# Strassen's seven products in the output projection, with weight sums made by adding DMAs

## The chip, the core and the metric

The kernel runs on one core of a Trainium2 chip. The metric is the device time of one execution, in microseconds (us). The median of three runs of the kernel before is 950.04 us (949.63 to 950.85).

## What is computed

A hybrid encoder block on x (1 x 512 x 2048, float32): adaLN-modulated RMSNorm, one input projection, dilated attention and a gated linear attention side by side, each times a SiLU gate. The change concerns what comes behind them:

```python
y = jnp.concatenate([a_out, g_out], axis=-1) @ w_out[layer]     # (512 x 2048) @ (2048 x 2048)
x = x + gate[:, None] * y
return rms_norm(x) * final_gain
```

## The kernel before, in words

Everything is float32, and a product is made of three matmuls in the `fp32r` form: each operand is split into a high half (rounded to that form) and a low half (what is left), and `three` (L205 to L208) adds high x high, low x high and high x low in PSUM. The high half of a weight tile is an ACT copy (L385), the low half a DVE subtraction (L369).

**The work in stages.** `unit` makes one projection of 512 output columns: four row or column tiles, 16 k tiles, three matmuls each, 192 matmuls of 128 x 512. The order of the units is qk2, qk4, qk6, gk, gv0, gv1, ag0, ag1, gg0, gg1 and then o0 to o3, the output projection. TensorE's order is the program's (`manual_schedule` for PE); DVE, ACT, POOL and SP are put in order by a scheduler, by priorities and dependencies, and `urgent` raises the priority of work that is put beside a unit (`side`, with the point in the unit at which each piece is issued).

**Weights.** A tile of weights is 128 x 2 x 512 (512 KB, two k tiles). `fetch` loads it from SP's queue into one of four ring slots (`raw`); `split_hi` and `split_lo` make the halves in one of three slots each (`whi`, `wlo`). A raw slot is free when the low half is made, a split slot when its last matmul is done. In a unit of the output projection one such tile feeds 24 matmuls (four row tiles x two k tiles x three), some 5.4 us.

**The operand.** The mixed and gated activations lie in four tiles `cat[0..3]`, 128 x 4 x 512 each: `cat[0]` and `cat[1]` are the attention half of the contraction (k tiles 0 to 7), `cat[2]` and `cat[3]` the other half. `cat_split` makes their halves: those of `cat[0]` and `cat[1]` beside the unit gg1, those of the others behind it, into the `h` tiles that held the normalised input (free when gg1 is done).

**The output.** After each of o0 to o2, `add_up` takes four PSUM tiles: DVE multiplies by the gate row `sb` (L1118) and adds x (L1119), ACT squares and sums (L1121), POOL multiplies by the final gain (L1123). The unit o3 runs as row tiles (0, 1), then 2, then 3, so that `finish` (ln, exp, scaling by DVE, ACT and POOL, four stores of 256 KB) of one lies beside the matmuls of the next; `finish_last` is what stands behind the last matmul. Five weight tiles of o3 are split early and kept.

**Queues.** SP issues all loads and stores but a few, in order; an issue that waits holds those behind it. POOL issues two small DMAs (L331) near the start. `gate_row` turns the gate into a row: a transposition on TensorE, an eviction by ACT, a DMA to memory and one back to all partitions (`sb`, 1 MB).

Of the kernel before, what the change touches and what calls it, by code (L numbers as in the profile page):

```python
# [18 lines left out]
P = 128  # L19
# [97 lines left out]

def _plan(tasks, free, ready):
# [52 lines left out]
def block_kernel(ctx: ExitStack, tc: tile.TileContext, a: dict):  # L171
# [5 lines left out]
    t2 = ctx.enter_context(tc.tile_pool(name="t2", bufs=16))  # L177
    gp = ctx.enter_context(tc.tile_pool(name="gp", bufs=2))
    sm = ctx.enter_context(tc.tile_pool(name="sm", bufs=4))
# [25 lines left out]
    def three(ps, lh, ll, rh, rl, first, last):  # L205
        mm(ps, lh, rh, start=first, stop=False)  # L206
        mm(ps, ll, rh, start=False, stop=False)  # L207
        mm(ps, lh, rl, start=False, stop=last)  # L208
# [111 lines left out]
    def row_part(j, i):  # L320
# [9 lines left out]
        if i:  # L330
# [6 lines left out]
    order = ["qk2", "qk4", "qk6", "gk", "gv0", "gv1", "ag0", "ag1", "gg0", "gg1",  # L337
             "o0", "o1", "o2", "o3"]
    gorder = [0, 1, 2, 3, 7, 4, 5, 6]
    uses = [(u, g) for u in order for g in (gorder if u == "o3" else range(KT // 2))]  # L340
    early = [("o3", g) for g in (0, 1, 2, 3, 7)]
    groups = []
    for u, g in uses:
        if (u, g) not in early:
            groups.append((u, g))
        if u == "o2" and 1 <= g <= 5:
            groups.append(early[g - 1])
    gi = {ug: i for i, ug in enumerate(groups)}
    upto = {}
    for i, ug in enumerate(uses):  # L350
        upto[ug] = max([gi[x] for x in uses[:i + 2]])
    raws, wts, low, c_h = {}, {}, set(), []

    def fetch(i):
        if i < len(groups) and i not in raws:
            u, g = groups[i]
            raws[i] = RAW(f"raw_{u}{g}", [2, 512])
            nc.sync.dma_start(raws[i], a["w_" + u][g])
# [13 lines left out]
    def split_hi(i):  # L372
        if i < len(groups) and i not in wts:
            fetch(i)
            u, g = groups[i]
            raw = raws[i].rearrange("p k c -> p (k c)")
            if u == "o3" and g < 4:
                dst = [t[:, 8 + 2 * g:10 + 2 * g, :].rearrange("p k c -> p (k c)") for t in c_h]
            elif u == "o3" and g == 7:
                dst = [gp.tile([P, 1024], F32R, tag="g", name=f"{u}{g}{e}") for e in "hl"]  # L380
            else:
                dst = None
            wts[i] = dst or (wp.tile([P, 1024], F32R, tag="whi", name=f"{u}{g}h"),
                             wp.tile([P, 1024], F32R, tag="wlo", name=f"{u}{g}l"))
            act(wts[i][0], raw, AF.Copy)  # L385
# [564 lines left out]
    def unit(name, natural, side=(), rhs=None, lr=None, tiles=range(4)):  # L950
# [3 lines left out]
        ps = [PJ(f"ps_{name}_{i}") for i in tiles]  # L954
        pos, tick, ticks = 0, 0, 16 * len(tiles)
        for q in range(KT // 2):
            g = gorder[q] if name == "o3" else q
            i0 = gi[name, g]
            todo = []
            if 0 in tiles:  # L960
                todo = list(range(gi[name, gorder[0] if name == "o3" else 0], upto[name, g] + 1))
                for i in todo:
                    split_hi(i)
                for ahead in (1, 2):
                    fetch(upto[name, g] + ahead)
            if i0 not in low:
                split_lo(i0)
            hi, lo = wts[i0]
            for n, i in enumerate(tiles):
                for kk in range(2):  # L970
                    k = 2 * g + kk
                    rh, rl = (h_hi[:, k, :], h_lo[:, k, :]) if rhs is None else rhs[k]
                    if natural:
                        t = slice(i * P, i * P + P)
                        cw = slice(kk * 512, kk * 512 + 512)
                        three(ps[n], rh[:, t], rl[:, t], hi[:, cw], lo[:, cw], q + kk == 0, q + kk == KT // 2)
                    else:
                        c = slice(kk * 512 + i * P, kk * 512 + i * P + P)
                        three(ps[n], hi[:, c], lo[:, c], rh, rl, q + kk == 0, q + kk == KT // 2)
                    tick += 1  # L980
                    if tick % (2 * len(tiles)) == 2:
                        for i_ in todo:
                            split_lo(i_)
# [5 lines left out]
            for i_ in todo:  # L989
                split_lo(i_)  # L990
# [77 lines left out]
    rhs = {}  # L1068

    def cat_split(k, hi, lo):  # L1070
        src = cat[k // 4][:, k % 4, :]
        act(hi, src, AF.Copy)
        tt(lo, src, hi.bitcast(F32), op=ALU.subtract)
        rhs[k] = (hi, lo)

    cs = []
    for j in range(2):
        cs.append((B8(f"ch{j}", [4, 512], F32R), B8(f"cl{j}", [4, 512], F32R)))
    side = [(0.1 + 0.08 * k, (lambda k=k: cat_split(k, cs[k // 4][0][:, k % 4, :], cs[k // 4][1][:, k % 4, :])))
            for k in range(8)]  # L1080
    ps = unit("gg1", False, side + some_sums("gg1"))
    gate_evict(ps, cat[3], "g1")
    for e in "hl":
        c_h.append(hp.tile([P, KT, 512], F32R, tag="h", name="c_" + e))
    for k in range(8):
        cat_split(8 + k, c_h[0][:, k, :], c_h[1][:, k, :])

    def gate_row():
# [3 lines left out]
        gt_ = sm.tile([KT, P], F32, tag="oh", name="gatet", bufs=1)  # L1092
        act(gt_, pg[:KT, :P], AF.Copy)
        garow = dp.tile([KT, P], F32, tag="garow", name="garow")
        nc.sync.dma_start(garow, gt_)
        nc.sync.dma_start(sb, bass.AP(garow.tensor, garow.offset, [[0, P], [1, D]]))

    x2, fgain = [], []
# [3 lines left out]
    def x_again(i):  # L1102
        def go():
            x2.append(B8(f"x2_{i}", [4, 512]))
            nc.sync.dma_start(x2[i].rearrange("p k c -> p (k c)"), a["x"][i * P:i * P + P, :])
        return go

    def gain_row(j):
        def go():
            fgain.append(T2(f"fgain{j}"))  # L1110
            nc.sync.dma_start(fgain[j], bass.AP(a["fgain"].tensor, a["fgain"].offset + 512 * j, [[0, P], [1, 512]]))
        return go

    def add_up(i, ps, j):

        x_ = x2[i][:, j, :]
        t = T2(f"y{i}{j}")
        tt(t, ps, sb[:, 512 * j:512 * j + 512], op=ALU.mult)  # L1118
        tt(x_, t, x_, op=ALU.add)  # L1119
        sq = T2(f"ysq{i}{j}")  # L1120
        act(sq, x_, AF.Square, accum_out=ssq[:, i, j:j + 1])  # L1121
        if j < 3:
            nc.gpsimd.tensor_tensor(x_, x_, fgain[j], op=ALU.mult)  # L1123

    for j in range(3):
        side = [(0.1 + 0.2 * i, x_again(i)) for i in range(4)] if j == 0 else []
        if j == 0:
            side += [(0.08, gate_row)] + [(0.15 + 0.2 * i, gain_row(i)) for i in range(4)]
        ps = unit(f"o{j}", True, side, rhs=rhs)
        for i in range(4):  # L1130
            add_up(i, ps[i], j)
    for i in range(4):

        tt(ssq[:, i, 0:1], ssq[:, i, 0:1], ssq[:, i, 1:2], op=ALU.add)
        tt(ssq[:, i, 0:1], ssq[:, i, 0:1], ssq[:, i, 2:3], op=ALU.add)
        nc.vector.tensor_scalar(ssq[:, i, 0:1], ssq[:, i, 0:1], 1.0 / D, EPS, op0=ALU.mult, op1=ALU.add)

    def finish(i, ps):

        add_up(i, ps, 3)  # L1140
        r = rn[:, i:i + 1]
        act(r, ssq[:, i, 3:4], AF.Ln, bias=ssq[:, i, 0:1], scale=1.0 / D)
        act(r, r, AF.Exp, scale=-0.5)
        x_ = x2[i]
        stt(x_[:, 3, :], x_[:, 3, :], r, fgain[3], op0=ALU.mult, op1=ALU.mult)
        act(x_[:, 0, :], x_[:, 0, :], AF.Copy, scale=r)
        nc.gpsimd.tensor_scalar(x_[:, 2, :], x_[:, 2, :], r, 1.0, op0=ALU.mult, op1=ALU.mult)
        act(x_[:, 1, :], x_[:, 1, :], AF.Copy, scale=r)
        for z in (3, 0, 2, 1):
            nc.sync.dma_start(a["out"][i * P:i * P + P, 512 * z:512 * z + 512], x_[:, z, :])  # L1150

    def finish_last(i, ps):

        add_up(i, ps, 3)
        r, x_ = rn[:, i:i + 1], x2[i]
        act(r, ssq[:, i, 3:4], AF.Ln, bias=ssq[:, i, 0:1], scale=1.0 / D)
        act(r, r, AF.Exp, scale=-0.5)

        def store(queue, z):
            queue.dma_start(a["out"][i * P:i * P + P, 512 * z:512 * z + 512], x_[:, z, :])  # L1160

        nc.vector.tensor_scalar(x_[:, 1, :], x_[:, 1, :], r, None, op0=ALU.mult)
        store(nc.sync, 1)
        act(x_[:, 0, :], x_[:, 0, :], AF.Copy, scale=r)
        stt(x_[:, 3, :], x_[:, 3, :], r, fgain[3], op0=ALU.mult, op1=ALU.mult)
        store(nc.sync, 0)
        act(x_[:, 2, :], x_[:, 2, :], AF.Copy, scale=r)
        store(nc.scalar, 2)
        store(nc.sync, 3)

    for tiles in ((0, 1), (2,), (3,)):
        ps = unit("o3", True, rhs=rhs, tiles=tiles)
        for i, p_ in zip(tiles, ps):
            if i < 3:
                finish(i, p_)
    with tc.manual_schedule(engines=PLANNED):
        finish_last(3, ps[0])
# [71 lines left out]
```

## Time and profile before

| | us |
|---|---|
| runs, median (lowest to highest) | 950.04 (949.63 to 950.85) |
| profiled execution, span from its first to its last instruction | 948.1 |
| first matmul of the output projection, from the span's start | 765.08 |
| last matmul | 939.09 |

The own time of the profiled execution isn't listed beside its span; the median of the runs is 1.9 us above the span. In the profile PE is TensorE's matmuls and PEld its weight loads (which overlap them), DVE is VectorE, ACT ScalarE, POOL GpSimd and SP the engine that issues most DMAs. A group's row gives line, engine, operation, output <- input, shape, count, then busy us and mean ns of one, then the idle time in front of it and what ended it. A row of the timeline begins with its start and its duration. L numbers are lines of the kernel before. In the windows, each engine's busy us and count of instructions are followed by the granted clock of TensorE (1.00 is full), the mean busy share of the 16 DMA engines and GB/s.

### The profile page before, as it was taken

The numbers are of one execution on the slowest core, as the hardware profiler recorded it, in microseconds if no ns is written. First come the engines' busy times: TensorE is split into PE (matmuls) and PEld (weight loads), VectorE is DVE, ScalarE is ACT, GpSimd is POOL, SyncE is SP. The second block draws the span as 40 slices with busy tenths as digits, with TensorE's granted clock in tenths as the row PEclk, the third lists the DMA queues.
The fourth block names the chain that finished last, engine by engine and source line by source line (L and its number), as shares of the span: only waits on it lengthen the run. The fifth ranks groups of instructions, "written<-read, shape, count | busy, mean of one in ns | idle before, by whom it ended". The sixth has DMA issues, their size and how long they took to land.

```text
span 948.1 us, 12029 instructions
## 1 busy us (share of the span) xinstructions
PE 935.1 (99%) x4471; PEld 777.2 (82%) x4471; DVE 604.6 (64%) x902; ACT 434.2 (46%) x732; POOL 78.7 (8%) x100
## 2 busy tenths in 40 slices
PE   8999999999999999999999999999999999999996
PEld 6888888888888888888878888888888888888885
DVE  7988899775656676766345665685975252446421
ACT  5553533655555655556215554453834151233222
POOL 0000000012022022121000000000010000202120
PEclk9999999999999999999999999999999999999999
DMA  9999496542423453532554243554565464344013
GB/s 348 403 411 376 186 359 251 156 135 102 126 92 106 147 200 109 175 128 94 163 172 130 87 156 111 178 177 145 181 202 183 141 222 148 102 144 154 23 50 128
DMA packets 45186, 163.63 MB, mean 173 GB/s; under 512 B 5733, under 2 KB 6021, under 8 KB 40393
## 3 DMA queue, kind: packets, MB, share of 16 engines
q1 hardware_dynamic: 44624, 162.25, 49.6%
q8 instruction: 35, 0.57, 0.3%
q10 hardware_dynamic: 440, 0.57, 0.2%
q14 instruction: 23, 0.18, 0.1%
q0 software_dynamic: 64, 0.07, 0.0%
HBM read 154.39 MB, written 4.28 MB: 167 GB/s over the span
## 4 chain that ended last, share of the span: by engine, by line
PE 96%; DMA 1%; DVE 1%; issue 1%; ACT 0%; SPq 0%; DVEq 0%
PE ps_o L206 6%; PE ps_o L208 6%; PE ps_o L207 6%; PE ps_qk L206 5%; PE ps_qk L208 5%; PE ps_qk L207 5%; PE o L711 3%; PE stb L208 3%; PE ps_gv L208 3%; PE ps_gv L207 3%; PE ps_ag L206 3%; PE ps_ag L208 3%; PE ps_gg L206 3%; PE ps_gg L207 3%; PE ps_gv L206 3%; PE ps_ag L207 3%
## 5 line engine op out<-in xcount | busy, mean ns | idle before, releaser
L305 DVE CUSTOM_DVE_ANT_0 cb<-cb,sb,c_bcond 128x2048 f32<-128x2048 f32 (+1 forms) x32 | 73.4, 2294 | 1.0 <-DMA cb<-in_wm 0.9
L680 ACT ACTIVATE p<-p,st 128x512 f32<-128x512 f32 x64 | 46.1, 721 | 55.6 <-DVE st L677 55.3
L685 POOL TENSOR_SCALAR p<-p,st 128x512 f32<-128x512 f32 x62 | 43.0, 694 | 332.6 <-DVE st L681 283.4
L702 DVE TENSOR_TENSOR pt<-t,pt 128x512 fp32r<-128x512 f32 x64 | 43.7, 688 | 15.6 <-ACT pt L701 15.4
L677 DVE CUSTOM_DVE_ANT_0 p<-s,g 128x512 f32<-128x512 f32 x64 | 43.6, 687 | 14.8 <-PE s L674 14.5
L701 ACT ACTIVATE pt<-t 128x512 fp32r<-128x512 f32 x64 | 37.8, 591 | 9.9 <-PE t L697 8.7
L697 PEld LDWEIGHTS t<-c_ident,p 128*128 128x128 f32 x256 | 31.5, 140 | 9.7 <-POOL p L685 1.4
L697 PE MATMUL t<-c_ident,p 128*128 128x128 f32 x256 | 38.5, 273 | 0.1
L711 PEld LDWEIGHTS o<-pt,vv 128*128 128x128 f32 x256 | 34.8, 188 | 2.8
L1123 POOL TENSOR_TENSOR x<-x,fgain 128x512 f32<-128x512 f32 x12 | 20.3, 1695 | 185.4 <-ACT ysq L1121 185.4
L711 PE MATMUL o<-pt,vv 128*128 128x256 f32 x256 | 35.6, 281 | 0.0
L1121 ACT ACTIVATE ysq<-x 128x512 f32<-128x512 f32 x16 | 10.1, 631 | 47.7 <-DVE x L1119 47.7
L873 POOL TENSOR_SCALAR dc<-st,sc 128x256 f32<-128x256 f32 x16 | 9.9, 617 | 249.2 <-DVE st L870 244.2
L305 DVE CUSTOM_DVE_ANT_0 rawg<-rawg,sb,gate 128x1024 f32<-128x1024 f32 x16 | 20.5, 1280 | 14.2 <-DMA rawg<-in_wg 14.2
L1118 DVE TENSOR_TENSOR y<-ps_o,sb 128x512 f32<-128x512 f32 x16 | 10.9, 682 | 25.9 <-PE ps_o L208 25.9
L681 DVE RECIPROCAL st<-st 128x1 f32<-128x1 f32 x64 | 10.3, 161 | 24.9 <-ACT p L680 24.8
L305 DVE CUSTOM_DVE_ANT_0 rawg<-rawg,sb,c_bcond 128x1024 f32<-128x1024 f32 x16 | 20.5, 1282 | 8.7 <-DMA rawg<-in_wg 8.7
L674 PE MATMUL s<-kl,qs 128*128 128x512 f32 x64 | 25.0, 391 | 0.0
L673 PE MATMUL s<-ks,qs 128*128 128x512 f32 x64 | 25.0, 390 | 0.0
L880 ACT ACTIVATE sq<-st,sc 128x256 f32<-128x256 f32 x24 | 12.2, 507 | 21.5 <-DVE st L870 11.9
L305 DVE CUSTOM_DVE_ANT_0 rawv<-rawv,shb,vbias 128x1024 f32<-128x1024 f32 x8 | 10.2, 1279 | 14.2 <-DMA rawv<-in_wv 14.2
L714 ACT ACTIVATE oh<-o 64x256 f32<-64x256 f32 x32 | 12.2, 381 | 13.7 <-PE o L711 12.6
(1289 smaller groups left out, 2920.7 us busy)
## 6 DMA issues: line engine op xcount, KB each, us to landing
cb<-in_wm SPq DMA_DIRECT2D x31, 1024.0 KB, 8.4
rawg<-in_wg SPq DMA_DIRECT2D x32, 512.0 KB, 3.6
raw_o<-in_w_o SPq DMA_DIRECT2D x32, 512.0 KB, 3.4
raw_qk<-in_w_qk SPq DMA_DIRECT2D x24, 512.0 KB, 3.3
rawb<-in_w_sb SPq DMA_DIRECT2D x16, 512.0 KB, 5.4
rawv<-in_wv SPq DMA_DIRECT2D x16, 512.0 KB, 4.1
raw_gv<-in_w_gv SPq DMA_DIRECT2D x16, 512.0 KB, 3.4
raw_ag<-in_w_ag SPq DMA_DIRECT2D x16, 512.0 KB, 3.3
```

What stands on the lines that cost most here:

```text
L206: mm(ps, lh, rh, start=first, stop=False)
L207: mm(ps, ll, rh, start=False, stop=False)
L208: mm(ps, lh, rl, start=False, stop=last)
L305: nc.vector.tensor_tensor_reduce(out=w, in0=w, in1=with_, op0=ALU.mult, op1=ALU.add, scale=1.0, scalar=init, accum_out=dst)
L673: mm(ps, qs[:, q], ks, start=True, stop=False)
L677: nc.vector.tensor_tensor_reduce(out=t, in0=ps, in1=gt[h][:, P * i:P * i + 512], op0=ALU.add, op1=ALU.min, scale=1.0, scalar=3e38, accum_o ...
L680: act(t, t, AF.Exp, bias=st[:, 0:1], scale=-1.0, accum_out=st[:, 1:2])
L685: nc.gpsimd.tensor_scalar(t, t, st[:, 2:3], 1.0, op0=ALU.mult, op1=ALU.mult)
L697: nc.tensor.transpose(pk[:, kt * P:kt * P + P], t[:, kt * P:kt * P + P], ident)
L701: act(hi, src, AF.Copy)
L702: tt(lo, src, hi.bitcast(F32), op=ALU.subtract)
L711: mm(po[:, :256], vv[h // 4][:, kt, h % 4, :], t[:, w, kt, :], start=kt == 0 and w == 0, stop=kt == 3 and w == 1)
```

## The change

The output projection is computed by one level of Strassen's algorithm (in Winograd's form). The operand A (512 rows x 2048) is cut into four blocks of 256 rows x 1024, and each of two pairs of column blocks of the weights (`OUT_PAIRS`, blocks 0 and 1, then 3 and 2, each 512 wide) into four blocks of 1024 x 512. For each pair seven products are made, in the order P1, P7, P6, P4, P5, P3, P2, each of two row tiles x 8 k tiles x three matmuls. P1, P6 and P5 add up in the same two PSUM tiles, P7 and P4 in two others; what a later block needs is kept in SBUF by ACT copies (`keep`).

*Block sums of weights.* `out_fetch` loads a block from SP and lets a DMA from POOL's queue add another block to the tile. P7's sum is made in four tiles of their own (`sum`); after P7's split the next DMA adds a block for P6 in place, and after P6's split one for P4. P5's sum is one load and one add in a ring tile. P1, P3 and P2 are plain loads. A weight tile now feeds 12 matmuls.

*Block sums of the operand.* DVE makes them: the differences for S3 in tiles of their own, S1, S2 and S4 in place in `cat`; each is split into halves (`halves`: ACT, then DVE, 1024 elements). A11 and S3 are split beside gg1, together with S1 and S2 of `cat[0]`; the others are put ahead of weight groups of the first pair's products (`later`).

*The end.* Each output tile gets a merge of PSUM and a kept tile on DVE, then gate, x and squares as before; the gain's multiplication moves from POOL to DVE. Rows 2 and 3 are finished behind P5 of the second pair, row 0 and then row 1 behind P2, which runs row by row. x is loaded again in halves, the gain in rows of two pairs. The pools for the middle of the kernel (`t2`, `gp`, `sm`) are closed behind gg1, and a pool `op` takes their place, whose tiles wait for the old tiles that they overlap.

```diff
+OUT_ORDER = ("P1", "P7", "P6", "P4", "P5", "P3", "P2")
+OUT_PAIRS = ((0, 1), (3, 2))
+OUT_WEIGHTS = {"P1": ("11", None), "P7": ("12", "22"), "P6": (None, "11"), "P4": (None, "21"),
+               "P5": ("11", "12"), "P3": ("22", None), "P2": ("21", None)}
...
+        load, add = OUT_WEIGHTS[prod]
+        if load is None:
+            t = sums_of[g]
+        elif prod == "P7":
+            t = sums_of[g] = op.tile([P, 2, 512], F32, tag="sum", bufs=4, name=f"sum{pair}{g}")
+        else:
+            t = RAW(f"raw_O{s}", [2, 512])
+        if load is not None:
+            j, z = block[load]
+            nc.sync.dma_start(t, a[f"w_o{j}"][z])
+        if add is not None:
+            j, z = block[add]
+            nc.gpsimd.dma_start(t, a[f"w_o{j}"][z], accum_op=ALU.add)
...
+    def keep(name, ps):
+            t = op.tile([P, 512], F32, tag="keep", bufs=7, name=f"{name}{n}")
+            act(t, p_, AF.Copy)
...
+    def add_up(i, j, merge, gain):
+        t = E_(f"y{i}{j}")
+        merge(t)
+        tt(t, t, sb[:, 512 * j:512 * j + 512], op=ALU.mult)
         tt(x_, t, x_, op=ALU.add)
-        sq = T2(f"ysq{i}{j}")
-        act(sq, x_, AF.Square, accum_out=ssq[:, i, j:j + 1])
-        if j < 3:
-            nc.gpsimd.tensor_tensor(x_, x_, fgain[j], op=ALU.mult)
+        act(t, x_, AF.Square, accum_out=ssq[:, i, j:j + 1])
+        if gain:
+            tt(x_, x_, fgain[j], op=ALU.mult)
...
+    with_ = {"P1": "A11", "P7": "S3", "P6": "S2", "P4": "A22", "P5": "S1", "P3": "S4", "P2": "A12"}
...
+    def product(pair, prod, ps, first, last, rows=(0, 1)):
+        ah, al = ops[with_[prod]]
+        for g in range(4):
+            s = (pair * len(OUT_ORDER) + OUT_ORDER.index(prod)) * 4 + g
+            i0 = gi["O", s]
+            ahead = 0 in rows
+            if ahead:
+                split_hi(i0)
+                split_hi(i0 + 1)
+                for n in (2, 3, 4):
+                    fetch(i0 + n)
+                split_lo(i0)
+                for go in todo.get((pair, prod, g), ()):
+                    go()
+            wh, wl = wts[i0]
+            for n in rows:
+                t = slice(P * n, P * n + P)
+                for kk in range(2):
+                    k = 2 * g + kk
+                    c = slice(512 * kk, 512 * kk + 512)
+                    three(ps[n], ah[:, k, t], al[:, k, t], wh[:, c], wl[:, c],
+                          first and k == 0, last and k == 7, not first)
+                if ahead and n == 0:
+                    split_lo(i0 + 1)
...
+    for z in range(2):
+        later(0, "P1", 2 * z, halves("S2", z, part(z, 0)))
+        later(0, "P7", 2 * z, halves("A22", z, part(2 + z, 1)))
+        later(0, "P6", 2 * z, halves("S1", z, part(z, 1)))
+        later(0, "P6", 2 * z + 1, lambda z=z: (to_s4(z), halves("S4", z, part(z, 0))()))
+    later(0, "P4", 0, a12)
+    for z in range(2):
+        later(0, "P4", 1 + 2 * z, lambda z=z: halves("A12", z, part(2 + z, 0))())
+    later(0, "P1", 1, gate_row)
+    later(0, "P4", 2, gain_rows(0))
+    later(0, "P4", 3, x_again(0))
+    later(1, "P6", 0, x_again(1))
+    later(1, "P6", 2, gain_rows(1))
+    for pair, (l, r) in enumerate(OUT_PAIRS):
+        product(pair, "P1", g1, True, True)
+        p1 = keep(f"p1{pair}", g1)
+        product(pair, "P7", gx, True, True)
+        p7 = keep(f"p7{pair}", gx)
+        product(pair, "P6", g1, False, True)
+        u2 = keep(f"u2{pair}", g1)
+        product(pair, "P4", gx, False, True)
+        for n in range(2):
+            add_up(2 + n, l, summed(gx[n], u2[n], ALU.add), True)
+        product(pair, "P5", g1, False, True)
+        v = keep(f"v{pair}", g1)
+        for n in range(2):
+            add_up(2 + n, r, negated(g1[n], p7[n]), not end)
+            if end:
+                finish(2 + n, r, first_squares(2 + n, [0, 1, l]))
+        product(pair, "P3", g2, True, True)
+        for n in range(2):
+            add_up(n, r, summed(g2[n], v[n], ALU.subtract), True)
+        if not end:
+            product(pair, "P2", g3, True, True)
+            for n in range(2):
+                add_up(n, l, summed(g3[n], p1[n], ALU.add), True)
+            continue
...
+        product(pair, "P2", g3, True, True, (0,))
+        add_up(0, l, summed(g3[0], p1[0], ALU.add), False)
+        finish(0, l, s[0])
+        product(pair, "P2", g3, True, True, (1,))
+        with tc.manual_schedule(engines=PLANNED):
+            add_up(1, l, summed(g3[1], p1[1], ALU.add), False)
+            finish_last(1, l, s[1])
```

More of the change, by code (lines that the diff above doesn't have):

```diff
@@ L334, in block_kernel @@
     h_lo = hp.tile([P, KT, 512], F32R, tag="h", name="h_lo")
[L337 to L347, printed above, removed]
+    order = ["qk2", "qk4", "qk6", "gk", "gv0", "gv1", "ag0", "ag1", "gg0", "gg1"]
+    groups = [(u, g) for u in order for g in range(KT // 2)]
+    groups += [("O", s) for s in range(2 * 4 * len(OUT_ORDER))]
     gi = {ug: i for i, ug in enumerate(groups)}
[L349 to L352, printed above, removed]
+    raws, wts, low, sums_of = {}, {}, set(), {}
     def fetch(i):
@@ new lines, in a12 @@
+    def a12():
+        operand("A12", [B8(f"A12{e}", [4, 512], F32R) for e in "hl"])
+    for z in range(2):
[4 more added lines that the diff above has]
+    later(0, "P4", 0, a12)
+    for z in range(2):
+        later(0, "P4", 1 + 2 * z, lambda z=z: halves("A12", z, part(2 + z, 0))())
```

250 lines of the change are left out of this document (141 added, 109 removed).

## The prediction, made before the changed kernel ran

> **What bounds the kernel now.** First the page: the busy line, the slices of the clock, and the chain that ended last.
>
> ```profile
> span 948.1 us, 12029 instructions
> ...
> PE 935.1 (99%) x4471; PEld 777.2 (82%) x4471; DVE 604.6 (64%) x902; ACT 434.2 (46%) x732; POOL 78.7 (8%) x100
> ...
> PEclk9999999999999999999999999999999999999999
> DMA  9999496542423453532554243554565464344013
> GB/s 348 403 411 376 186 359 251 156 135 102 126 92 106 147 200 109 175 128 94 163 172 130 87 156 111 178 177 145 181 202 183 141 222 148 102 144 154 23 50 128
> ...
> PE 96%; DMA 1%; DVE 1%; issue 1%; ACT 0%; SPq 0%; DVEq 0%
> ```
>
> TensorE is busy 99% of the span at its full granted clock, and 96% of the chain is TensorE. A matmul taken away is worth its time, as long as TensorE stays the last to be ready. So I read the stage that is changed, by windows (columns: busy us of PE, PEld, DVE, ACT, POOL, then clock, DMA share, GB/s), and its first and last matmul in the timeline.
>
> ```profile
> 765.00:798.00 33.00, 33.00 (x148) 27.20 (x147) 13.03 (x16) 12.61 (x18) 0.00 (x0) 1.00 0.64 223
> 798.00:831.00 33.00, 33.00 (x148) 27.31 (x147) 14.56 (x14) 9.40 (x15) 6.88 (x4) 1.00 0.29 96
> 831.00:864.00 33.00, 33.00 (x147) 27.35 (x146) 20.87 (x22) 12.74 (x19) 7.42 (x4) 1.00 0.46 151
> 864.00:896.00 32.00, 32.00 (x143) 26.49 (x142) 11.61 (x12) 7.97 (x9) 1.19 (x1) 1.00 0.24 76
> 896.00:939.20 43.20, 43.20 (x192) 35.66 (x190) 13.56 (x22) 10.69 (x25) 8.33 (x7) 1.00 0.20 73
> ```
>
> ```profile
> 765.08 0.39 PE L206 MATMUL ps_o<-o00h,ch 128*128 128x512 f32 x1
> ...
> 939.09 0.39 PE L208 MATMUL ps_o<-o36l,c_h 128*128 128x512 f32 x1
> ```
>
> The output projection runs from 765.08 (below: T) to 939.09 without a gap: 768 matmuls, (939.09 - 765.08) / 767 = 0.2269 us each. DVE is busy 42% and the DMA engines 20 to 64% there. There is room beside TensorE, and the question is how much of it the change uses up.
>
> **What the change removes.** Seven products for eight, each 2 row tiles x 8 k tiles x 3 matmuls = 48, and two column pairs: 672 matmuls for 768. The built program agrees: 3760 rows on TensorE for 3856. 96 x 0.2269 = 21.8 us less. A product takes 48 x 0.2269 = 10.9 us, a pair of columns 76.2 us.
>
> **What it adds: DMA.** A weight tile now serves 12 matmuls (2.7 us), not 24, and block sums are loaded too. For 32 loads of 512 KB come 40 plain loads and 32 adds (16 of each pair's), issued by POOL in order, one waiting for the split in front of it. No add is in the trace of before. The nearest rows:
>
> ```profile
> raw_o<-in_w_o SPq DMA_DIRECT2D x26, 512.0 KB, 3.3
> x<-in_x SPq DMA_DIRECT2D x2, 1024.0 KB, 7.1
> sb<-garow SPq DMA_DIRECT2D x1, 1024.0 KB, 7.4
> ...
> DMA  6589921343033332175535555300000000029041
> GB/s 236 200 264 330 381 69 80 120 124 120 0 120 120 120 120 79 54 230 158 201 123 184 177 161 199 82 37 0 6 0 0 0 0 0 0 103 379 1 173 67
> ```
>
> (The lower two lines are slices of 765 to 940 alone.) Where the engines are busy in nine tenths or more they move 381 GB/s here and 411 in the page's third slice: 524,288 bytes take 1.28 to 1.37 us of all sixteen, and I take 1.32. An add can't move less than a load: lower end 1.32. It has the weights to read, the old tile to read and the sum to write. If the reading of the two goes one after the other it is two loads, 2.64, and with the write in series as well three, 3.96. I take 2.64: of the rows above, sixteen engines already run near their best with one stream of reads, so a second stream has to queue. Landing of an add: 3.3 + 1.3, about 4.6 us.
>
> By the Trainium skill, "Collectives: The Full Stack", section "The bandwidth ceiling: the fold count and why AG ≠ RS ≠ AR", an add in the DMA engine costs no cycles of its own but takes two source reads on one ring, measured there as a ratio of 1.93. No row of before can show it; by it an add is an estimated 2.55 us, and the sum below +3.8 us instead of +6.3. It speaks against the change all the same, since a bare byte count sees an add as one load.
>
> **Pair 1, the DMA term.** When can the first add go? P5's first weights (loaded early) take the ring slot of P1's first tile, which is free when that tile's low half is made:
>
> ```profile
> 755.49 1.23 DVE L369 TENSOR_TENSOR o00l<-raw_o,o00h 128x1024 fp32r<-128x1024 f32 x1 [4.21 <-ACT o00h L385]
> 756.74 5.77 SPq L358 DMA_DIRECT2D raw_o<-in_w_o  x2
> ```
>
> So it is loaded from 756.74 and lands 3.3 later, at 760.0 = T - 5.0; POOL's first add goes then. The last add that P4 needs must land before P4's last weight group starts, T + 3 x 10.9 + 8.2 = T + 40.9, less the two halves of the split:
>
> ```profile
> L385 ACT ACTIVATE c_h<-raw_o 128x1024 fp32r<-128x1024 f32 x4 | 4.2, 1056 | 4.2 <-DMA raw_o<-in_w_o 4.2
> L369 DVE TENSOR_TENSOR c_l<-raw_o,c_h 128x1024 fp32r<-128x1024 f32 x4 | 4.9, 1220 | 1.9 <-ACT c_h L385 1.9
> ```
>
> 1.06 + 1.22, so T + 38.4 or 43.4 us after the first add. In that time POOL's queue holds, in this order: two adds of P5, four of P7, four of P6, one of P5, two of P4, one of P5, two of P4: 16 x 2.64 = 42.2 us. SP's queue beside it loads one P5 tile, the four sum tiles, sb (1 MB), two P5 tiles, 0.5 MB of gains, 2 MB of x: 14 x 1.32 = 18.5 us. 60.7 - 43.4 = **17.3 us** late. Nor can the queue be kept full: P6's first add waits for P7's first split, P4's for P6's, each a gap of about the shortest landing in the trace (2.2 us, of 128 KB from SBUF to SBUF): **4.4 us**, between 0 and 9.
>
> ```profile
> DMA to landing us min/median/max: 2.2/2.2/3.3
> ```
>
> **Pair 2.** P7's sum tiles are free after P4, so their loads and adds lie under P5 to P1 (16 loads and 4 adds, 31.7 us in 43.6). Left are 12 adds and some 8 loads (x, gains, three of P5) from just before P1 to the same point 38.4 us in: 12 x 2.64 + 8 x 1.32 = 42.2 against 39.4: **2.8 us**.
>
> **DVE and ACT.** DVE in pair 1: 28 low halves x 1.22 = 34.2; ten low halves of the operand blocks and four in-place sums, all of 1024 elements, 14 x 1.22 = 17.1; eight merges of four instructions (merge, gate, add, gain) of 0.69 = 22; 73.3 us of 76.2. The rows:
>
> ```profile
> L1119 DVE TENSOR_TENSOR x<-y,x 128x512 f32<-128x512 f32 x15 | 17.3, 1155 | 0.3
> L1118 DVE TENSOR_TENSOR y<-ps_o,sb 128x512 f32<-128x512 f32 x16 | 10.9, 682 | 25.9 <-PE ps_o L208 25.9
> ```
>
> Both have the same shape; the add at L1119 was slow (1155 ns) only beside POOL's gain multiply, which now is on DVE, so I charge 0.69. DVE thus is nearly full, and what it loses, TensorE loses: I take **2 us** (0 to 5), at the low halves queued behind a merge of six instructions after P5 and P3. Pair 2 has no operand blocks: 56 us of 76.
>
> ACT at the start: the gate's last silu, then the table load, two weight halves (1.06 each, the second after P1's first group), the gate's eviction, and six operand halves before it comes to P7's first weights.
>
> ```profile
> 765.59 0.58 ACT L999 ACTIVATE sgg<-ps_gg 128x512 f32<-128x512 f32 x1
> 766.19 1.28 ACT L203 ACT_TABLE_LOAD   x1
> ...
> 767.48 3.76 ACT L1072 ACTIVATE c_h<-cat 128x512 fp32r<-128x512 f32 x7
> ```
>
> From the row at 767.48 = T + 2.4: +1.06 +0.25 +1.06 + 6 x 1.06 = T + 11.1, P7's high half at T + 12.2, its low half at T + 13.4. P1 ends at T + 10.9: 2.1 us of stall. In the forecast it lies inside the 17.3, since it delays the deadline too; where adds are cheap it counts by itself.
>
> **The end.** P2 of pair 2 goes row by row, 1.36 us a group. Its fourth weights' low half stands on DVE behind P3's merges: 6 x 0.69 + 1.22 = 5.4 after P3, wanted at 4.1 + 0.45: 0.9 us. Behind the last matmul:
>
> ```profile
> 939.52 0.69 DVE L1118 TENSOR_TENSOR y<-ps_o,sb 128x512 f32<-128x512 f32 x1 [7.30 <-PE ps_o L208]
> 940.24 0.69 DVE L1119 TENSOR_TENSOR x<-y,x 128x512 f32<-128x512 f32 x1
> 940.97 0.63 ACT L1121 ACTIVATE ysq<-x 128x512 f32<-128x512 f32 x1 [8.16 <-DVE x L1119]
> ...
> 943.64 0.38 ACTq L1160 DMA_DIRECT2D out<-x  x1
> ```
>
> this chain stays and gets one merge more, 0.7. Together **1.6 us**. What moves ahead of T (two differences, four splits, two sums on DVE, 10 us for 5.5) lies beside the last gate projection, where DVE idles 4.2 us before each split (the row at 755.49): nothing.
>
> **Sum** against the profiled span: -21.8 + 17.3 + 4.4 + 2.8 + 2 + 1.6 = +6.3. The median of the three runs, 950.04, is 1.9 above the span (start and end around it, not changed); 950.0 + 6.3, rounded: **956.5 us**.
>
> **Rivals.**
> 1. *Adds are cheap: TensorE stays the bound, and it is faster.* For it: DMA share 0.20 to 0.64 in the windows. With an add at one load, 16 x 1.32 + 18.5 = 39.6 fits into 43.4. Left are 2.1 + 2 + 1.6 against 21.8: **934 us**. By the sum, forecast and gain part at 16a + 18.5 - 43.4 = 14 or a = 2.4 us, 1.8 loads. Chance 0.28 for adds under 1.5 loads.
> 2. *Adds are dear, in the engines or on POOL.* At three loads: pair 1 38.5, pair 2 18.7, with 4.4 and 3.6, less 21.8: **993 us**. POOL alone would do it with over 43.4 / 16 = 2.7 us for each issue; the row below (16 partitions, where an add has 128) speaks against it, but only by a factor of four. Chance 0.24.
>
> ```profile
> L331 POOL DMA_DIRECT2D grow<-bias x2: 497/594/692, 53.1 to 64.1; - x2
> ```
>
> 3. *TensorE runs no fewer matmuls.* The built program excludes it; with all else that I overlook, 0.02.
>
> The forecast (adds of 1.5 to 2.4 loads) has 0.46 and by the same sum its own range 943 to 971; 0.14 of it lies below, 0.06 within 0.2% (about what a measurement of this kernel can tell from no change), 0.26 above. Faster: 0.14 + 0.28 = 0.42. Same: 0.06. Slower: 0.26 + 0.24 + 0.02 = 0.52. The range goes from rival 1's price to rival 2's, 934 to 994, and leaves out dearer adds still, about 0.14, and 0.03 below.
>
> **What will show it.** Right: in the 45 us after T the DMA share is over 0.9, and TensorE's gaps end with P7's to P4's weights, whose high halves on ACT wait for DMA; the matmul pitch stays 0.227; from P5 of pair 1 few gaps. Rival 1: DMA share under 0.8 there, landing of adds under 5 us, one gap at P7's start. Rival 2: landings above 9 us, or POOL's issue above 2.7 us. I am wrong in kind if the gaps end with DVE and no DMA stands behind them, or if loads slow down beside adds by more than their bytes.

## The result, and the profile after

The median went from 949.84 us (four runs) to 966.1 us (four runs, 964.77 to 969.8): a ratio of 1.0175 (95% interval 1.0155 to 1.0195), 16.3 us slower. The forecast was 6.5 us slower, 956.5. The profiled execution of after is the one of 969.8 us, the slowest of its four; the other three have spans of 963.0 to 964.4.

The page of after, the lines that answer to those of before (the last two of the middle block are the DMA queues: q1 is fed by SP, q0 by POOL, and q0's 16.84 MB are the 32 adds):

```profile
span 968.0 us, 12067 instructions
...
PE 929.5 (96%) x4375; PEld 763.7 (79%) x4375; DVE 656.0 (68%) x960; ACT 470.7 (49%) x770; POOL 85.7 (9%) x120
...
PEclk9999999999999999999999999999999989999898
DMA  9999596533432644534453353445444599979863
GB/s 354 401 413 374 198 349 228 157 117 104 128 104 75 196 156 136 162 107 142 145 170 112 107 167 134 156 156 170 152 153 138 174 265 250 270 249 242 173 200 148
...
q1 hardware_dynamic: 46352, 166.44, 49.3%
q0 software_dynamic: 4672, 16.84, 8.9%
...
PE 78%; DMA 9%; DVE 6%; issue 4%; ACT 2%; POOL 1%; SPq 0%; ACTq 0%; DVEq 0%; POOLq 0%
```

TensorE did 96 matmuls fewer, and its share of the chain fell from 96% to 78%; DMA rose from 1% to 9%. In four of the last eight slices the DMA engines are as busy (9) as when they move 400 GB/s early in the kernel, but move some 240 to 270. Now the stage by windows cut at the starts of products (columns as in the prediction's windows). First come P1 to P4 of pair 1 in two rows, then P5, P3 and P2, then P1 of pair 2, P7 and P6, and the rest:

```profile
768.70:812.30 43.60, 36.26 (x139) 26.25 (x138) 28.64 (x26) 23.90 (x27) 13.03 (x15) 0.92 1.03 261
812.30:834.40 22.10, 15.93 (x58) 11.14 (x56) 7.72 (x7) 7.24 (x9) 2.61 (x4) 0.92 0.99 269
834.40:868.00 33.60, 33.26 (x145) 26.86 (x144) 28.91 (x39) 17.02 (x26) 0.86 (x1) 1.00 0.84 249
868.00:878.90 10.90, 10.90 (x49) 9.02 (x49) 9.35 (x14) 6.08 (x9) 3.51 (x5) 1.00 0.84 238
878.90:912.70 33.80, 27.16 (x98) 20.58 (x97) 9.28 (x8) 10.40 (x12) 7.01 (x8) 0.85 1.06 246
912.70:958.20 45.50, 43.73 (x193) 35.73 (x191) 36.06 (x51) 25.89 (x43) 4.32 (x3) 1.00 0.44 144
```

The DMA share is about 1 (1.03 and 0.99) from the start of the stage to the end of P4, and again in P7 and P6 of pair 2 (1.06). TensorE's waits in this stretch (us in total, times, longest), and the landing time of the adds:

```profile
PE gx L213 <- ACT O4h L403: 4.8, 1, 4.8
PE gx L213 <- ACT O14h L403: 3.8, 1, 3.8
PE g L213 <- ACT O36h L403: 3.7, 1, 3.7
PE g L213 <- ACT O38h L403: 2.4, 1, 2.4
PE g L215 <- DVE O55l L389: 1.8, 1, 1.8
```

```profile
L377 POOL DMA_DIRECT2D sum<-in_w_o x24: 853/862/1392, 772.8 to 908.7; - x24
...
DMA to landing us min/median/max: 5.3/11.5/18.1
```

O4 is P7's first weight group, O14 the third of P4; O36 and O38 belong to P6 of pair 2, O55 is the fourth of the last product. All but the last name a high half on ACT, which itself waited for an add (ACT waited 9.9 us for O36's). POOL issues an add in 0.86 us in the middle and 1.39 at the most, so the issue isn't the price; an add lands after 11.5 us in the middle, 5.3 at the least.

Matmuls of the stage in order of time: the first one; two of P7's first group, behind the 4.8 us gap, and one of its second; the first of pair 2's P1 and of its P4; the last one:

```profile
768.70 0.39 PE L213 MATMUL g<-O0h,A11h 128*128 128x512 f32 x1
...
787.41 0.63 PE L214 MATMUL gx<-O4h,S3l 128*128 128x512 f32 x1
787.84 0.63 PE L215 MATMUL gx<-O4l,S3h 128*128 128x512 f32 x1
...
791.49 0.39 PE L213 MATMUL gx<-O5h,S3h 128*128 128x512 f32 x1
...
868.04 0.39 PE L213 MATMUL g<-O28h,A11h 128*128 128x512 f32 x1
...
912.65 0.39 PE L213 MATMUL gx<-O40h,c_h 128*128 128x512 f32 x1
...
958.01 0.39 PE L215 MATMUL g<-O55l,A12h 128*128 128x512 f32 x1
```

Behind the gap the pitch is 0.43 us, not 0.227, and the window of these 5 us has a granted clock (third column from the end) of 0.50:

```profile
784.75:790.10 5.35, 4.92 (x11) 3.44 (x12) 2.59 (x3) 2.36 (x4) 1.56 (x2) 0.50 1.05 299
```

So TensorE lost time in two ways: waits, and slow matmuls behind them. The terms, from the starts of the products in the profiled execution (a product without a gap takes 10.89 us; 958.24 is one pitch after the start of the last matmul):

| Part | Forecast | Measured | How |
|---|---|---|---|
| matmuls removed | -21.8 | -21.8 | 672 of 768, same pitch where there is no gap |
| ahead of the stage | 0 | +3.6 | first matmul 768.70 for 765.08 |
| pair 1, P1 to P4 | 17.3 + 4.4 | +22.1 | 768.70 to 834.40, less 4 products |
| pair 1, P5, P3, P2 | 2 | +1.0 | 834.40 to 868.04, less 3 |
| pair 2, P1, P7, P6 | 2.8 | +11.9 | 868.04 to 912.65, less 3 |
| pair 2, P4 to P2, and the tail | 1.6 | +2.0 +1.0 | 912.65 to 958.24, less 4; 968.0 - 958.0 for 948.1 - 939.1 |

The sum is +19.8, the spans differ by 19.9; the medians, 16.3. Pair 1 came out at the size that was worked out; pair 2 did not.

### The profile page after: what moved, and what is told of

It is laid out like the page before. It is cut to its first block, busy times and chain, and to the rows that moved or that the text cites. A ratio compares the mean times of both kernels' runs of the same rounds, so it can differ in the third digit from the quotient of the medians.

```text
span 968.0 us, 12067 instructions
## 1 busy us (share of the span) xinstructions
PE 929.5 (96%) x4375; PEld 763.7 (79%) x4375; DVE 656.0 (68%) x960; ACT 470.7 (49%) x770; POOL 85.7 (9%) x120
## 3 DMA queue, kind: packets, MB, share of 16 engines
q1 hardware_dynamic: 46352, 166.44, 49.3%
q0 software_dynamic: 4672, 16.84, 8.9%
## 4 chain that ended last, share of the span: by engine, by line
PE 78%; DMA 9%; DVE 6%; issue 4%; ACT 2%; POOL 1%; SPq 0%; ACTq 0%; DVEq 0%; POOLq 0%
DMA sum<-in_w_o 5%; PE ps_qk L213 5%; PE ps_qk L215 5%; PE ps_qk L214 5%; PE o L729 3%; PE stb L215 3%; PE ps_gv L215 3%; PE ps_gv L214 3%; PE ps_gv L213 3%; PE stb L214 3%; PE t L715 3%; PE stb L213 3%; PE ps_ag L215 3%; PE ps_ag L213 3%; PE ps_ag L214 3%
## 5 line engine op out<-in xcount | busy, mean ns | idle before, releaser
L695 DVE CUSTOM_DVE_ANT_0 p<-s,g 128x512 f32<-128x512 f32 x64 | 43.6, 687 | 15.2 <-PE s L692 14.9
L377 POOL DMA_DIRECT2D sum<-in_w_o x24 | 21.5, 919 | 67.4 <-DMA sum<-in_w_o 38.6
L699 DVE RECIPROCAL st<-st 128x1 f32<-128x1 f32 x64 | 10.3, 161 | 24.9 <-ACT p L698 24.9
L898 ACT ACTIVATE sq<-st,sc 128x256 f32<-128x256 f32 x24 | 12.2, 507 | 18.6 <-DVE st L888 10.4
L736 DVE TENSOR_TENSOR cat<-o,oh 64x256 f32<-64x256 f32 x32 | 13.3, 416 | 8.2 <-ACT oh L732 7.8
L467 ACT ACTIVATE h_hi<-xt,shift 128x512 fp32r<-128x512 f32 x16 | 11.5, 719 | 13.0 <-DVE shift L312 13.0
## 6 DMA issues: line engine op xcount, KB each, us to landing
sum<-in_w_o POOLq DMA_DIRECT2D x24, 512.0 KB, 11.9
```

Source lines behind the costliest of these rows:

```text
L695: nc.vector.tensor_tensor_reduce(out=t, in0=ps, in1=gt[h][:, P * i:P * i + 512], op0=ALU.add, op1=ALU.min, scale=1.0, scalar=3e38, accum_o ...
```

## The experiments

Theory A: the adds fill the DMA engines, at about two loads each, and all else is small; what pair 2 lost above the forecast comes from the place of P5's adds in POOL's queue. Theory B: the waits come from DVE, ACT and the order of splits and merges. References: 949.84 us before, 966.1 after.

**No adds.** The adding DMA is left out (L377):

```diff
-            nc.gpsimd.dma_start(t, a[f"w_o{j}"][z], accum_op=ALU.add)
+            pass
```

> The changed kernel without its 32 adding DMAs: P7 and P5 only load their first block, P6 and P4 use P7's tile again, so the block sums are left out. Theory A (the adds' DMA time is the loss): the gaps in P7 to P4 of both pairs go, what stays is the stall ahead of the stage (about 3.6 us), ACT's backlog at P7 (2.1), DVE (1) and the end (3) against the 21.8 us of matmuls: 937 to 941 us. Theory B (the waits come from DVE, ACT and the order of the splits, the DMAs only stand in front of them): little changes, 955 us or more.

932.28 us (931.66 to 933.34). B falls: without the adds the change would win 17.5 us (ratio 0.9815, 0.98 to 0.983), and the adds cost 966.1 - 932.3 = 33.8. It is even below A's 937 to 941: some of my small terms were too large (pair 1 loses 0.5 us in all). From the first matmul, 767.01, the first 43.6 us of this run:

```profile
767.00:810.60 43.60, 43.46 (x192) 35.55 (x191) 35.55 (x32) 31.04 (x35) 0.00 (x0) 1.00 0.62 216
```

DVE and ACT do the same work as in the first two rows of after, in 43.6 us instead of 65.7, and TensorE is busy for 43.46 of them: DVE at 82% and ACT at 71% stop nothing.

**Plain loads in place of the adds**, same queue, place and tile:

```diff
-            nc.gpsimd.dma_start(t, a[f"w_o{j}"][z], accum_op=ALU.add)
+            nc.gpsimd.dma_start(t, a[f"w_o{j}"][z])
```

> Each adding DMA is a plain load of the same block, from the same queue, to the same tile, at the same place, so the block sums are left out. Theory A1 (it is the adding that costs, about 2.7 us of the sixteen engines for 1.5): the DMA work of pair 1 up to the last weights of P4 falls from 65 to some 45 us, which just fits: 941 to 947 us. Theory A2 (it is the second block's transfer as such, POOL's queue and the chain of waits through it): as the changed kernel, 960 to 966 us.

942.13 us (938.44 to 943.17), as A1 has it. Of the 33.8 us, 9.9 are the second block's transfer and 24.0 the adding. The prediction's sum had no such 9.9: by it, adds at the price of a load fit in and cost nothing, but here P1 to P4 of pair 1 lose 6.4 us and P1, P7 and P6 of pair 2 lose 5.1. The same bytes on POOL's queue now take

```profile
q0 software_dynamic: 4672, 16.84, 5.0%
```

of sixteen engines' span: 0.050 x 941.3 / 32 = 1.47 us for a plain load, against 0.089 x 968.0 / 32 = 2.69 us for an add, a ratio of 1.83. The forecast's 2.64 was right. A rival is that all packets take longer in fuller engines. The other queue's don't: in the kernel without adds q1 has

```profile
q1 hardware_dynamic: 46352, 166.44, 52.2%
```

which is 486 us of 931.6; in after the same packets take 49.3% of 968.0, 477 us. So by packet time loads don't slow down beside adds; that they would was one of the signs that the prediction named for being wrong in kind.

The Trainium skill ("Collectives: The Full Stack", "The bandwidth ceiling: the fold count and why AG ≠ RS ≠ AR") puts the cost of an add down to its two reads, with a ratio of 1.93 between two collectives. The ratio of packet times here lies 5% below it; that the two reads are the reason, no run here shows.

**POOL in the written order.** P5's adds then come behind P4's in both pairs:

```diff
+    ctx.enter_context(tc.manual_schedule(engines={E.Pool}))
     for pair, (l, r) in enumerate(OUT_PAIRS):
```

> POOL issues the adds in the written order: P5's four come behind P4's, not ahead of P6's. Theory A with the queue's order (in pair 2 three of P5's adds, 8 us of DMA time, stand ahead of P6's first): pair 2 loses 7 to 9 us of its 12, pair 1 stays within 2 us: 957 to 960 us. Rival (the DMA engines are full for the whole of P7 to P4 and the order can't matter): 965 to 967 us.

961.07 us (960.94 to 962.37), 5 less than after, where 6 to 9 were expected. In its profile P1, P7 and P6 of pair 2 lose 2.1 us instead of 11.9; P4 to P2 lose 3.9 instead of 2.0. Pair 1 loses 24.4 instead of 23.1, only later: 12.5 in P1 to P4 and 11.9 in P5, P3 and P2, where its own adds are now late. Pair 1 is short of DMA time in both orders of its adds; pair 2 is not.

**Pair 2's order alone**, with pair 1 as it was:

```diff
         end = pair == 1
+        if end:
+            ctx.enter_context(tc.manual_schedule(engines={E.Pool}))
```

> The changed kernel with one thing moved: in pair 2 alone POOL issues P5's four adds behind P4's; pair 1 and all other queues are as they were. Theory A with the queue's order (pair 2's 12 us come from P5's adds standing ahead of P6's, and these can't start before P7's splits, 4 to 5 us into P1): 7 to 10 us less than the changed kernel, 956 to 959 us, with gaps of pair 2 under 3 us in all. Rival (pair 2 is short of DMA time as a whole, by 12 adds and 8 loads, wherever they stand): 963 us or more.

960.36 us (959.84 to 961.18): 5.7 less than after by the medians, not quite the 7 to 10 expected, and 8.4 less from first to last matmul in the two profiled executions (180.9 us for 189.3). P1, P7 and P6 of pair 2 lose 1.5 us, not 11.9, at the same number of adds and loads, so the rival (too little DMA time in pair 2 as a whole) falls. The gaps of pair 2 in all are 5.7 us, not the under 3 expected: P4 to P2 lose 4.1 instead of 2.0, since P5's adds now come later. First matmuls of P1 and P4 here, and the windows of P7 and P6:

```profile
866.40 0.39 PE L213 MATMUL g<-O28h,A11h 128*128 128x512 f32 x1
...
900.58 0.39 PE L213 MATMUL gx<-O40h,c_h 128*128 128x512 f32 x1
...
876.50:887.40 10.90, 10.90 (x50) 9.03 (x49) 4.03 (x4) 3.89 (x5) 3.49 (x4) 1.00 1.03 229
887.40:899.80 12.40, 11.73 (x50) 8.76 (x49) 3.83 (x4) 5.21 (x6) 2.92 (x5) 1.00 1.06 250
```

The engines are as full as in after (share 1.03 and 1.06), but with the adds that are wanted next. POOL in after (pair 2 begins at 868.04):

```profile
872.41 0.86 POOL L377 DMA_DIRECT2D raw_O<-in_w_o  x1 [33.78 <-DMA raw_O<-in_w_o]
873.56 0.86 POOL L377 DMA_DIRECT2D raw_O<-in_w_o  x1 [0.29 <-issue]
877.11 0.88 POOL L377 DMA_DIRECT2D raw_O<-in_w_o  x1 [2.69 <-DVE ssq L1196]
877.67 2.11 POOL L377 DMA_DIRECT2D sum<-in_w_o  x2
886.57 0.86 POOL L377 DMA_DIRECT2D raw_O<-in_w_o  x1 [6.79 <-DMA raw_O<-in_w_o]
```

and here (pair 2 begins at 866.40):

```profile
874.87 0.86 POOL L377 DMA_DIRECT2D sum<-in_w_o  x1 [37.81 <-DVE ssq L1196]
877.22 0.86 POOL L377 DMA_DIRECT2D sum<-in_w_o  x1 [1.49 <-DVE O33l L389]
...
899.20 3.88 POOL L377 DMA_DIRECT2D raw_O<-in_w_o  x4
```

`raw_O` are P5's adds, wanted (without gaps) 44 us into the pair, when four products are done; `sum` are P6's, wanted 22 in. In after three of P5's go first, 8 us of DMA time, and O36's high half starts at 892.57, 14.9 us behind its add's issue. What also shows: neither kernel starts P6's adds before some 8 us into the pair (8.5 here, 9.6 in after), since they go into P7's tiles when P7's low half has read them (O32l ends at 876.0 in after), and that half takes a weight slot that P1 has to free.

**The side work ahead of the stage.** In after, TensorE waits at the transposes of the stage before, and DVE shows why: the scheduler put the two differences for S3 ahead of the decay chain.

```profile
673.61 1.22 DVE L1103 TENSOR_TENSOR diff<-cat 128x1024 f32<-128x1024 f32 x1
674.75 0.69 DVE L837 TENSOR_TENSOR g<-g,e 128x512 f32<-128x512 f32 x1
675.35 1.22 DVE L1103 TENSOR_TENSOR diff<-cat 128x1024 f32<-128x1024 f32 x1
```

```profile
PE kt L869 <- DVE ki L859: 2.0, 1, 2.0
```

```diff
-    ps = unit("gg1", False, side + some_sums("gg1"))
+    with tc.manual_schedule(engines={E.DVE, E.Activation}):
+        ps = unit("gg1", False, side + some_sums("gg1"))
```

> DVE and ACT take the last gate projection's side work (operand halves, differences, sums) in the written order, so that the two differences no longer run ahead of the decay chain of the stage before. If the 2.0 us stall at the transposes of ki and the lower clock behind it are the change's: the first matmul of P1 is 2.5 to 3.6 us earlier and the time 962 to 964 us. If the stall is one execution's chance, or if the DMA stage swallows what is won ahead of it: 965 to 967 us.

The wait goes and the first matmul of P1 is at 764.54, 4.2 us earlier, but the time is 965.97 us (965.73 to 966.88): the same. Two things can hide the gain, and this run doesn't tell them apart. In part it is waited for: the wait for O4 is 6.1 us instead of 4.8, O36's 4.2 for 3.7, and from first to last matmul the stage takes 0.9 us more (190.2 for 189.3). In part the late start is after's profiled execution alone: it is the slowest of its four, and its span is 3.3 us longer than the one here (968.0 for 964.7).

**Is the low clock a loss of its own?** Spare matmuls fill the gaps ahead of O4 (22) and O14 (18); nothing uses their result:

```diff
+    FILL = {4: 22, 14: 18}
...
+            if s in FILL:
+                spare = PJ(f"spare{s}")
+                for _ in range(FILL[s]):
+                    mm(spare, s3[:, 0, 0:P], s3[:, 1, :], start=True, stop=True)
```

> The changed kernel with 22 spare matmuls (5.0 us) ahead of P7's first weights of pair 1 and 18 (4.1 us) ahead of P4's third, where TensorE waited 4.8 and 3.8 us and then ran for some 5 us at half speed; their result is used by nothing. Theory A (the DMAs set when pair 1's P4 ends): the matmuls behind run at full speed, the time won is waited for at the next weights, 964 to 968 us. Rival (the low clock after a gap is a loss of its own, 2 to 3 us at each place): 960 to 962 us.

967.27 us (966.75 to 967.87). The number is in A's range, but the run has a flaw. The longest waits are now

```profile
PE g L213 <- ACT O11h L403: 5.5, 1, 5.5
PE g L213 <- ACT O36h L403: 3.9, 1, 3.9
PE gx L213 <- ACT O7h L403: 1.6, 1, 1.6
```

and the second filling is

```profile
827.31 4.24 PE L1260 MATMUL spare<-S3h 128*128 128x512 f32 x18
```

O14's low half had ended at 826.2, so here these 18 matmuls filled no gap, and some 4.1 us of the time are theirs. Without them the run would take an estimated 963 us, between the two ranges. At O4 the filling did what it should: the matmuls behind it run at a pitch of 0.227 and a granted clock of 1.00, and the time that TensorE keeps there is waited for at O7 and O11, where the clock falls to 0.50 again (816 to 822 us). The last high half of P4 (O15) starts 60.8 us after the stage's first matmul, 60.4 in after. So the slow matmuls behind O4 lay inside the DMAs' time; whether those behind a last gap, such as O14's in after, cost time of their own stays open.

The Trainium skill ("TensorE: Matmul & The Clock Gate", "HAM oscillation — how this bites in real kernels") counts the slow matmuls behind a DMA wait as a penalty added to it. The half clock agrees with the granted 0.50 here; that it adds to the wait is not borne out at O4.

**An add by itself.** In the kernel without adds, POOL issues four plain loads and then four adds on free tiles behind pair 2's P5:

```diff
-            nc.gpsimd.dma_start(t, a[f"w_o{j}"][z], accum_op=ALU.add)
+            pass
...
+            for n in range(4):
+                nc.gpsimd.dma_start(probe[n], a["w_o0"][n])
+            for n in range(4):
+                nc.gpsimd.dma_start(probe[n], a["w_o1"][n], accum_op=ALU.add)
```

> The kernel without adds (932.3 us), with a probe where the DMA engines are quiet, behind pair 2's P5: POOL issues four plain loads of 512 KB into free tiles, then four adding DMAs into the same tiles; nothing reads them. By the packet times of the runs so far (2.7 us of the sixteen engines for an add, 1.5 for a load from the same queue) the four loads land within 8 us and the four adds within 14 us of their first issue, an add alone in some 5. Rival (an add costs no more than a load by itself and is slow only beside other traffic): four adds within 8 us.

Inconclusive (936.14 us, one run). The place was not quiet (DMA share 0.97 to 1.08 from 905 to 920 us): the adds, issued from 906.1 to 913.0, ran beside stores of the output and landed after 9.8 to 12.5 us, the plain loads after 5.2 to 10.3. An add alone stays unmeasured; the least landing in any run is 5.2 us.

**Versions with less DMA work.** If full DMA engines are the loss, fewer bytes should give time back, at most the 21.8 us. P1's tiles of block 11 are kept; DVE makes P6's sums from them, P5's sum is made in them, and POOL has the written order:

```diff
+        if prod == "P6":
+            t = sums_of[g]
+            tt(t, t, first_of[g], op=ALU.add)
+            return t
+        if prod == "P5":
+            t = first_of[g]
+            load = None
...
+            if prod == "P1":
+                first_of[g] = t
...
+    ctx.enter_context(tc.manual_schedule(engines={E.Pool}))
```

> A version after what the first four showed: P1's tiles of block 11 are kept, DVE adds them to P7's sums for P6 (eight additions of 1.2 us), P5's sum is made in P1's tile by an adding DMA, and POOL keeps the written order. Per pair there are 12 adds instead of 16, 16 plain loads instead of 20, and only 8 adds (21 us of the sixteen engines) with 11 loads (16) have to land before P4's last weights, in 43 us. Theory A (full DMA engines are the loss): most gaps of P7 to P4 go in both pairs, P5 keeps some 3 us, the stall ahead of the stage and the end stay: 937 to 945 us, faster than before the change. Rival (DVE, then 78 of 76 us in pair 1, becomes the bound): gaps that end with low halves on DVE, 948 us or more.

949.44 us (948.31 to 952.31; ratio to before 0.9996, 0.9987 to 1.0005): 16.7 less than after, yet above the 937 to 945 expected. P6 and P4 of pair 1 and all of pair 2 have no gap above 0.5 us until the last weights, but P7 loses 6.3 and P5 10.4. TensorE's longest wait there is for DVE, which looks like the rival, but DVE itself is waiting for a DMA:

```profile
825.98 0.69 DVE L1190 TENSOR_TENSOR x<-y,x 128x512 f32<-128x512 f32 x1 [3.96 <-DMA x<-in_x]
829.16 0.69 DVE L1190 TENSOR_TENSOR x<-y,x 128x512 f32<-128x512 f32 x1 [2.48 <-DMA x<-in_x]
829.77 1.22 DVE L398 TENSOR_TENSOR O18l<-raw_O,O18h 128x1024 fp32r<-128x1024 f32 x1
```

The loads of x went out together with four adds, and O18's low half stands behind the merges that need x. Next, the side work's order of above, and the last product's low halves at a higher priority:

> The version before with two edits: the last gate projection's side work in the written order on DVE and ACT (as in the run of that order alone), and the low halves of the last product ahead of the merges on DVE. If the stage is no longer bound by DMAs, what is won ahead of it (1 to 2 us) and at the last weights (1.5 to 2 us) now counts: 2 to 4 us less than the version before. If DMAs still bind it: within 1 us of it.

947.66 us, 1.8 less, just short of the 2 to 4: in the profiles the stage starts 1.4 us earlier and the last product loses nothing instead of 1.6, and of these 3.0 us more than half now counts. The two edits were not run apart. Ratio to before 0.9974 (0.9965 to 0.9983). Then pair 1's merges of P4 written behind P5's splits:

> The last version, with pair 1's merges of P4 written behind P5's splits: in that version P5's third low half stood on DVE behind two additions of x that waited for the loads of x (4.1 and 2.1 us of DVE's waiting, 8.2 us of TensorE's). If this wait on DVE's queue is what P5 loses: 4 to 8 us less, 940 to 944 us. If P5's own adds, which share the engines with x, are late as well: 1 to 3 us less.

947.24 us, 0.4 less: a miss. P5 lost 6.4 instead of 10.3, but P3 3.4 and P2 1.3 instead of 0 and 0.7; the queue on DVE had only stood in front of late DMAs. Then the sums' tiles laid where no late reader holds them, and fetched at a higher priority, so that P7's loads go before P1 begins:

```diff
+    for tag, bufs in (("keep", 7), ("e", 3), ("fg", 2)):
+        op.tile([P, 512], F32, tag=tag, bufs=bufs, name="lead_" + tag)
...
+                    early = s + n in (4, 5, 6, 7)
+                    with tc.high_priority(offset=EARLY) if early else nullcontext():
+                        fetch(i0 + n)
```

> The same, and the sums' tiles lie where no late reader of the old pools holds them, with their loads and adds at a higher priority, so that P7's first loads no longer wait for the last gate's merges at the start of P1. Theory A (full DMA engines in the 20 us after the start of P1 are what P7 loses, 6.5 us): 4 to 6 us less than with the late merges alone. Rival (P7's first weights wait for ACT's backlog and DVE): within 1 us of it.

942.0 us, 5.2 less, as A has it; ratio to before 0.9914 (0.99 to 0.9929). Last, SP's queue of pair 1 in the written order from P6 on, with pair 2's sum tiles loaded at the start of P2:

```diff
+            ordered.enter_context(tc.manual_schedule(engines={E.SP}))
...
+            for s in range(32, 36):
+                fetch(gi["O", s])
             product(pair, "P2", g3, True, True)
```

> The version of 942.0 us with SP's queue of pair 1 in the written order from P6 on, and pair 2's four sum tiles loaded at the start of pair 1's P2: in the version before, these loads and one of their adds (9 us of DMA time) ran between x and P5's adds. Theory A (in P5 and P3 of pair 1 the engines are still full, 9 us of gaps): 3 to 6 us less, 936 to 939 us. Rival (what P5 waits for is the order on DVE behind the loads of x): within 1 us.

938.45 us (937.24 to 940.37), 3.6 less, as A has it: 1.2% faster than before (ratio 0.9881, 0.9866 to 0.9897). P5, P3 and P2 of pair 1 lose 0.5 us instead of 9.4. Its longest waits in the whole stage:

```profile
PE g L215 <- DVE O31l L398: 1.7, 1, 1.7
PE g L215 <- DVE O30l L398: 1.5, 1, 1.5
```

At P1 of pair 2, which lost nothing in the version before, 4.9 us are left; the DMA share there is 1.05 (842 to 853 us).

## Why the prediction was half right

- **The bound and the sign.** Right, and the time lies in the forecast's own range, 943 to 971; but that range was made for the price of an add, which isn't what moved the time. TensorE bounded the kernel before; the change made the DMA engines the bound in P7 to P4, with the waits at P7's and P4's high halves on ACT and the DMA share over 0.9, as "what will show" had it.
- **The price of an add**, 2.64 us. Right: 2.69 by the packets, by which the same sum gives some 958 us. Rival 2 (three loads, or POOL's issue) falls: 0.86 us an issue in the middle. But its sign, "landings above 9 us", was badly chosen: the median is 11.5, since landing counts the queue in front of the add, not its price.
- **Pair 1**, 17.3 + 4.4. Right in sum: 22.1 measured. The 17.3, DMA work that doesn't fit, has its mechanism shown by the runs without adds and with plain loads. The 4.4 came out by luck: it was to be gaps in the queue ahead of P6's and P4's first adds, but from 780 to 827.5 us the DMA share is 1.06, without a gap. The engines stood idle earlier, for some 2.4 us (share 0.85 from the first add at 764.25 to 780), and the DMA work up to 827.5 came to some 64 us of the sixteen engines, where 60.7 were counted.
- **Pair 2**, 2.8 us. This step failed. It counted 12 adds and 8 loads "from just before P1 to the same point 38.4 us in", as if the engines could work on them all that time in any order. They could not start: P5's first add went 4.4 us into P1, P6's 9.6 us, as P7's tiles have to be read first. And the scheduler had put three of P5's adds, not wanted before the fifth product, ahead of P6's. 11.9 was measured, so "from P5 of pair 1 few gaps" was wrong too; with that order alone undone it was 1.5. The time was then 5.7 us lower, which is over half of the 9.8 us by which the change cost more than forecast (16.3 for 6.5).
- **Ahead of the stage**, nothing. Wrong in itself: DVE's 4.2 us of idleness ahead of each split was real, but the scheduler moved the differences into the stage before, onto the decay chain; 1.0 to 3.6 us (first matmul at 766.1 to 768.7 in the eight profiles that keep that order, after's the latest, 765.08 before). It was not what the median hung on: moved back, the time stayed at 965.97.
- **DVE, ACT and the end.** DVE 2 and ACT's 2.1 were too large: 1.0 in the profile, and at most 0.6 at P7's start without adds. The end was too small: 3.0 for 1.6, P2's fourth low half alone 1.8 for 0.9. In the sum DVE's term and the end's nearly cancel, which is luck.
- **"The matmul pitch stays 0.227".** Wrong behind gaps (0.43). At O4 that had no cost of its own; elsewhere no run shows it.
- **Rival 1**, 934 us for adds at the price of a load. Its own case is the run with plain loads, 942.13: eight more, since work that fits by the sum still left 11.5 us of gaps. The kernel without adds took 932.28; there the rest of the sum comes out within 2 us, but with a late start (1.9) in place of ACT's and DVE's terms.

What stays open: how the remaining 4 us of the miss divide between the end, the late start and pair 1 in the median run, since after's only trace is of its slowest execution (spans from 963.0 to 968.0).

## What to carry to other kernels

Price an adding DMA as about two loads of the same size (1.83 here), and don't stop at the sum: for each add write down when its tile is free, when its result is wanted, and what its queue holds in front of it. A stretch that has enough DMA time in total still stalls when work that is wanted late stands ahead of work that is wanted soon, and a saving ahead of a DMA-bound stretch was worth nothing here (965.97 for 966.1 us). A block that is loaded for one product and kept for the next sums saves a load and an adding DMA, at 1.2 us of a DVE that had room: with that, and the queues in the order of need, Strassen's seven products beat the eight.

## What the runs showed of the hardware that was not expected

- POOL issues an adding DMA in 0.86 us in the middle and a plain load of the same shape in 0.53; adds that follow each other closely took up to 2.2 us each (POOL in the written order).
- With adds among the loads, sixteen engines at a share of 0.99 to 1.06 move 246 to 269 GB/s in three windows of 22 to 44 us; early in the kernel, before the first add, up to 413.
- The packets of the plain loads took no longer beside adds: 477 us of sixteen engines for 486 without.
- After a gap of 4.8 us the granted clock was 0.50 for some 5 us.
